# A decoder layer on one core: seven products instead of eight in the middle groups of the down projection, with sums of weight quarters made in memory

## The chip, the cores and the metric

One core of one Trainium2 chip runs the whole kernel. The metric is the device time of one execution in microseconds (us); lower is better.

## The reference, cut to what matters

The reference computes one step of a decoder layer for 512 prompt tokens and 64 sample tokens (576 in all), model width 1024, in float32: a mixer (gated linear attention and retention in parallel, four heads each), cross-attention into 256 memory tokens, and a squared-ReLU MLP of width 4096. Only the MLP's arithmetic is rearranged by the change; the mixers get transfers to issue.

```
hf = rmsnorm(x, g_pre_ffn)
x = x + rmsnorm(jnp.square(jax.nn.relu(hf @ w_up)) @ w_down, g_post_ffn)     # w_up 1024x4096, w_down 4096x1024
```

## The kernel before

Activations lie with features on the 128 partitions and the 576 tokens along the free axis, in two halves of 288. Every float32 matrix is held as a high part and a low part in the float32r format (a cast on ScalarE, `L93`, and a subtraction on VectorE, `L94`), and each product is three matmuls: high by high, low by high, high by low (`mm3`, `L251` to `L253`). A plain product of one block of 128 output features (`gemm_m`) is 8 input blocks, 3 matmuls and 2 halves: 48 matmuls of 128x128 by 288 columns.

Weights come as tiles of 128x1024 (512 KB). `plan` is the order of all of them, written out by hand. `wfetch` issues the next load on SyncE's queue (SP, `L180`) into one of four buffers `wraw`; `wsplit` makes `wh` and `wl`, of which there are three each; `wnext` keeps two split tiles ready. A load waits until the tile four before it has been split.

The kernel runs in stages: memory keys and values, mixers, mixer output projection, cross-attention, MLP. In the mixers, eight units (`UNITS`: four heads, each once for retention and once for gated attention) take eight plain products each from `plan`, and between them `tick()` advances generators in `side` that do the attention of the unit in small pieces. GpSimd (POOL) does rotary additions, causal masks, powers of -0.5 (`rs`, `L874`) and parts of the gates there.

The MLP runs in four groups `g` of 1024 hidden features. Group 0 uses plain products, up (`project`) and down (`gemm_m`). For groups 1 to 3 the up projection uses a seven-product scheme of Winograd's kind: the token halves and the parity of the feature blocks cut activations and weights in quarters, and `sevenfold` makes four output quarters out of 7 products, each 12 matmuls of 288 columns (4 blocks, 3 matmuls), instead of 8. It needs sums of activation quarters (`fsh`, `fsl`, made once by `sums_f`) and sums of weight quarters, which `begin` makes with four VectorE subtractions (`L213`) per block out of two loaded tiles. There are four blocks `b` to a group. Three accumulators are used (`acc` in pool psa, `b` in pso, `c` in psg); a product that goes on in an accumulator waits until the copy that reads its earlier content is done. `c1` and `c2` (tiles `hr`) collect the quarters, then ReLU and square on ScalarE (`L713`, `L717`, `L718`, `L722`, `L723`), then the split into `hh` and `hl`.

The down projection of groups 1 and 2 has 8 plain products, each added to `y3` in memory on chip by VectorE (`L654`). That of group 3 is in `last`, with the final norm, by halves.

The framework keeps the data's order but may place instructions on an engine's queue in another order than the one in which they are written.

Of the kernel before, what the change touches and what calls it, by code (L numbers as in the profile page):

```python
# [26 lines left out]


RING, STAY, RAW, SEVEN = 0, 1, 2, 3
# [29 lines left out]
def decoder_step(ctx, tc, xT, memT, ktc, vc, s_gla, s_ret, w_in, w_ga, w_a2, w_mix, w_xq, w_xk, w_xv, w_xo,  # L59
                 w_up, w_ups, w_down, vecs, cst, gam, y_out, mk_out, mv_out, sg_p, sr_p, sg_s, sr_s):  # L60
# [48 lines left out]
    def h2(ap):  # L109
        return ap.rearrange("p (a t) -> p a t", a=2)  # L110
# [24 lines left out]
    def whole(w, b0=0):  # L135
        return [t for b in range(4) for t in wtiles(w, b0 + b)]
# [9 lines left out]
    def rest(ts, n):  # L146
        return ts[2 + n:6] + ts[:2]
# [15 lines left out]
    def seven(w, b0):  # L163
        return [(w[b0 + b][:, kh], SEVEN) for b in range(4) for kh in range(2)]
# [6 lines left out]
    wq = []  # L171
    units = []

    def wfetch():
        if plan and sum(m == SEVEN for _, m in raws) < 2:
            src, mode = plan.pop(0), RING
            if isinstance(src, tuple):
                src, mode = src
            raw = wp.tile([P, 1024], F32, name="wraw", bufs=N_RAW)
            nc.sync.dma_start(out=raw if len(src.shape) == 2 else raw.rearrange("p (k n) -> p k n", n=src.shape[2]), in_=src)  # L180
            raws.append((raw, mode))

    def wsplit():
        if units:
            units.pop(0)()
        elif raws:
            if raws[0][1] == SEVEN:
                begin()
                return
# [4 lines left out]
            pool = staying[-1] if mode == STAY else wp  # L194
            wh = pool.tile([P, 1024], F32R, name="wh")
            wl = pool.tile([P, 1024], F32R, name="wl")
            split(wh, wl, raw)
            ready.append((wh, wl))

    def halves(w):  # L200
        return w.rearrange("p (q n) -> p q n", q=2)

    def begin():


        while len(raws) < 2:
            wfetch()
        p0, p1 = (raws.pop(0)[0] for _ in range(2))
        t = wp.tile([P, 1024], F32, name="wraw", bufs=N_RAW)
        q0, q1, qt = halves(p0), halves(p1), halves(t)  # L210

        def minus(out, a, b):
            nc.vector.tensor_tensor(out=out, in0=a, in1=b, op=ALU.subtract)  # L213

        def ring(raw):
            wh = wp.tile([P, 1024], F32R, name="wh")
            wl = wp.tile([P, 1024], F32R, name="wl")
            split(wh, wl, raw)
            ready.append((wh, wl))

        def own(raw, o, n):
            w = wq[0][:, o:o + n], wq[0][:, o + n:o + 2 * n]
            split(*w, raw)
            ready.append(w)

        def unit_a():
            ring(p0)
            wfetch()

        units.extend([unit_a, lambda: ring(t), lambda: own(p1, 0, 1024),  # L230
                      lambda: minus(q1[:, 0], q1[:, 0], qt[:, 0]), lambda: own(q1[:, 0], 2048, 512)])
        minus(qt[:, 1], q1[:, 1], q0[:, 1])
        minus(q0[:, 1], q0[:, 1], q0[:, 0])
        minus(qt[:, 0], q1[:, 1], q0[:, 1])
        wfetch()

    def wnext(n=P):

        while sum(len(r) == 2 for r in ready) < 2 and (raws or plan):
            while not units and plan and len(raws) + sum(len(r) == 1 for r in ready) < N_RAW - 1:  # L240
                n0 = len(raws)
                wfetch()
                if len(raws) == n0:
                    break
            if not raws and not units:
                break
            wsplit()
        return [a.rearrange("p (k n) -> p k n", n=n) for a in ready.pop(0)]
# [24 lines left out]
    def sevenfold(x, p1, p5, u2, c11, c22, c12, c21):  # L273
# [11 lines left out]
        def more():  # L285
            if units:
                wsplit()

        while len(ready) < 3:
            wsplit()  # L290
# [3 lines left out]
        p1(acc)  # L294
        while units:
            wsplit()
        wd = ready.pop(0)
        prod(c, wa, 1, "S1", True)
        p5(c)
        if raws and raws[0][1] == SEVEN:  # L300
            begin()
        prod(acc, wc, 0, "S2", False)
        wsplit()
        u2(acc)
        prod(b, wb, 0, "A12", True)
        more()
        c11(b)
        prod(acc, wc, 1, "S3", False)
        c22(acc)
        prod(c, wb, 1, "S4", False)  # L310
        c12(c)
        more()
        prod(acc, wd, 0, "A22", False)
        more()
        c21(acc)
# [332 lines left out]
    xnp = ctx.enter_context(tc.tile_pool(name="xnp", bufs=2))  # L648
# [4 lines left out]
    def add(out, a, b, op=ALU.add):  # L653
        nc.vector.tensor_tensor(out=out, in0=a, in1=b, op=op)  # L654

    def sums_f():

        for j in range(4):
            c1, c2 = (hp.tile([P, 2, NH], F32, name="hr") for _ in range(2))
            for i, c in enumerate((c1, c2)):  # L660
                q = slice(2 * i, 2 * i + 2)
                add(c, f32(fh[:, q, j]), f32(fl[:, q, j]))
            yield
            add(c2[:, 1], c2[:, 0], c2[:, 1])
            add(c2[:, 0], c1[:, 0], c2[:, 0], ALU.subtract)
            add(c1[:, 0], c2[:, 1], c1[:, 0], ALU.subtract)
            add(c1[:, 1], c1[:, 1], c1[:, 0], ALU.subtract)
            yield
            split(fsh[:, 2:4, j], fsl[:, 2:4, j], c2)
            split(fsh[:, 0:2, j], fsl[:, 0:2, j], c1)  # L670
            yield

    FQ = {"A11": (fh, fl, 0), "A12": (fh, fl, 1), "A22": (fh, fl, 3),
          "S2": (fsh, fsl, 0), "S4": (fsh, fsl, 1), "S3": (fsh, fsl, 2), "S1": (fsh, fsl, 3)}

    def xf7(n):
        h, l, q = FQ[n]
        return h[:, q], l[:, q]

    y3 = None  # L680
    for g in range(4):
        hh = acta.tile([P, 4, 4, NH], F32R, name="hh", tag="xh")
        hl = acta.tile([P, 4, 4, NH], F32R, name="hl", tag="xl")

        if g == 0:
            lows = []
            for half in range(2):
# [14 lines left out]
                while lows:  # L702
                    lows.pop(0)()
            y3 = bigb.tile([P, KT, NT], F32, name="y3", tag="res")
            side.append(sums_f())
            wq.append(biga.tile([P, 4608], F32R, name="wq", tag="biga"))
        else:
            for b in range(4):
                c1, c2 = (hp.tile([P, 2, NH], F32, name="hr") for _ in range(2))

                def c22(ps):
                    add(c2[:, 1], ps, c2[:, 1])
                    nc.scalar.activation(c2[:, 1], c2[:, 1], AF.Relu)  # L713

                def c12(ps):
                    add(c1[:, 1], ps, c1[:, 1])
                    nc.scalar.activation(c1, c1, AF.Relu)  # L717
                    nc.scalar.activation(c1, c1, AF.Square)  # L718
                    split(hh[:, 0:2, b], hl[:, 0:2, b], c1)

                def c21(ps):
                    nc.scalar.activation(c2[:, 0], ps, AF.Relu)  # L722
                    nc.scalar.activation(c2, c2, AF.Square)  # L723
                    split(hh[:, 2:4, b], hl[:, 2:4, b], c2)

                sevenfold(xf7, lambda ps: nc.scalar.copy(c1[:, 0], ps), lambda ps: nc.scalar.copy(c2[:, 1], ps),
                          lambda ps: nc.scalar.copy(c1[:, 1], ps), lambda ps: add(c1[:, 0], ps, c1[:, 0]), c22, c12, c21)
        if g < 3:
            for k in range(KT):
                ps = gemm_m(quarters(hh, hl), None)  # L730
                y = h2(y3[:, k, :])
                if g == 0:
                    nc.scalar.copy(y, ps)
                else:
                    add(y, ps, y)
                tick()
            drain()

# [42 lines left out]
def mixers(tc, env):  # L781
    e = Env(env)
    nc, split, split_p, gtile, atile, gemm_m, mm3, f32, h2, tick, side = (
        e.nc, e.split, e.split_p, e.gtile, e.atile, e.gemm_m, e.mm3, e.f32, e.h2, e.tick, e.side)
# [3 lines left out]
    with ExitStack() as st:  # L788
# [103 lines left out]
        def unit(h, ret, second, finish):  # L892
# [40 lines left out]
            else:  # L933
                nc.vector.tensor_tensor(out=q2(kf), in0=ps[:, :, :256], in1=pv(em), op=ALU.mult)
                for g in range(2):
                    nc.vector.tensor_tensor(out=kd[:, g], in0=parts(ps[:, g, 256:]), in1=parts(sv(em)[:, g]), op=ALU.mult)

# [7 lines left out]

            oT = u3.tile([P, 2, NT], F32, name="oT")
# [169 lines left out]
            for m in range(2):  # L1116
# [5 lines left out]
                tick()  # L1122
            for m in range(2):
# [4 lines left out]
                tick()  # L1128

# [292 lines left out]
```

## Time and profile before

| | |
|---|---|
| time, median of 3 runs | 1206.34 us (1204.42 to 1206.52) |
| the profiled execution's own time | 1206.06 us |
| its span, first to last instruction | 1204.3 us |
| TensorE (PE) busy | 1172.6 us, 97% |
| VectorE (DVE) / ScalarE (ACT) / GpSimd (POOL) busy | 745.9 / 564.3 / 152.8 us |
| moved by DMA | 158.37 MB, mean 131 GB/s |

The profile shows one execution. Times are in us unless marked ns; PEclk is the clock granted to TensorE in tenths of full speed; a DMA share is the busy share of the 16 DMA engines. Matmuls overlap each other, so the duration of one (some 295 ns) is more than the distance between two.

### The profile page before, as it was taken

To read this page: it belongs to the slowest core of one execution; us is meant where nothing else is said; L and a number is where in the kernel's file an instruction comes from. 1 tells how busy PE (TensorE), PEld (TensorE's weight loads), DVE (VectorE), ACT (ScalarE), POOL (GpSimd) and SP (SyncE) were. 2 spreads that over 40 slices of the span, in tenths; PEclk is the share of its full clock that TensorE was granted. 3 is DMA by queue.
4 is the path that set the end of the run, shared out by engine and by line. 5 is a ranking of instruction groups with operands and counts; after the bars stand their busy time and mean duration, and the time that the engine had idled before them with its cause. 6 is when DMAs were issued, how large, how long until landed. Compare 5 with 4: busy or idle time off the path is not lost.

```text
span 1204.3 us, 21958 instructions
## 1 busy us (share of the span) xinstructions
PE 1172.6 (97%) x9006; PEld 1140.8 (95%) x9006; DVE 745.9 (62%) x1332; ACT 564.3 (47%) x992; POOL 152.8 (13%) x165
## 2 busy tenths in 40 slices
PE   8999999999999999999999999999999999999995
PEld 7999999999999999999999877989999999999995
DVE  6756556565756575658677544686847457555665
ACT  6624455533544344434565444556437316415652
POOL 0621213131312231221001000000000000000000
PEclk9999999999999999999999999999999999999998
DMA  7852324242324242422644676654322322422641
GB/s 268 277 195 90 125 70 130 79 136 80 127 80 127 88 128 71 142 75 91 213 150 138 232 252 233 196 160 127 105 71 87 107 70 65 129 71 70 199 145 60
DMA packets 65621, 158.37 MB, mean 131 GB/s; under 512 B 5648, under 2 KB 34448, under 8 KB 65392
## 3 DMA queue, kind: packets, MB, share of 16 engines
q1 hardware_dynamic: 65520, 156.96, 40.9%
q8 instruction: 71, 1.16, 0.4%
q14 instruction: 30, 0.25, 0.1%
HBM read 140.68 MB, written 16.25 MB: 130 GB/s over the span
## 4 chain that ended last, share of the span: by engine, by line
PE 86%; DVE 6%; DMA 3%; ACT 3%; issue 1%; POOL 1%; SPq 0%; POOLq 0%; DVEq 0%; ACTq 0%
PE psg L252 23%; PE psg L251 23%; PE psg L253 23%; PE psa L281 4%; PE psg L281 2%; PE psa L251 1%; DVE wl L94 1%; PE psa L252 1%; PE psa L253 1%; PE pso L281 1%; DMA wraw<-in_w_xo 1%; PE pso L1241 1%; DMA wraw<-in_w_down 1%; PE psa L1084 1%; ACT wh L93 1%; DVE res L526 1%
## 5 line engine op out<-in xcount | busy, mean ns | idle before, releaser
L251 PE MATMUL psg<-xh,wh 128*128 128x288 f32 x1296 | 386.6, 298 | 3.2 <-ACT wh L93 3.2
L252 PE MATMUL psg<-xh,wl 128*128 128x288 f32 x1296 | 383.6, 296 | 2.5 <-DVE wl L94 2.5
L253 PE MATMUL psg<-xl,wh 128*128 128x288 f32 x1296 | 383.1, 296 | 0.0
L94 DVE TENSOR_TENSOR wl<-wraw,wh 128x1024 fp32r<-128x1024 f32 x197 | 243.8, 1238 | 89.9 <-ACT wh L93 88.9
L93 ACT CAST wh<-wraw 128x1024 fp32r<-128x1024 f32 x197 | 206.9, 1051 | 164.5 <-PE psg L253 104.6
L251 PEld LDWEIGHTS psg<-xh,wh 128*128 128x128 f32 x1296 | 244.3, 189 | 5.5 <-ACT wh L93 4.1
L252 PEld LDWEIGHTS psg<-xh,wl 128*128 128x128 f32 x1296 | 244.6, 189 | 3.3 <-DVE wl L94 3.2
L253 PEld LDWEIGHTS psg<-xl,wh 128*128 128x128 f32 x1296 | 244.4, 189 | 0.1
L251 PE MATMUL psg<-hh,wh 128*128 128x288 f32 x512 | 151.9, 297 | 0.7 <-DVE y L760 0.6
L252 PE MATMUL psg<-hh,wl 128*128 128x288 f32 x512 | 150.7, 295 | 0.3 <-DVE wl L94 0.3
L253 PE MATMUL psg<-hl,wh 128*128 128x288 f32 x512 | 150.7, 295 | 0.0
L251 PEld LDWEIGHTS psg<-hh,wh 128*128 128x128 f32 x512 | 96.1, 188 | 1.6 <-issue 1.1
L252 PEld LDWEIGHTS psg<-hh,wl 128*128 128x128 f32 x512 | 96.1, 188 | 0.6 <-DVE wl L94 0.6
L253 PEld LDWEIGHTS psg<-hl,wh 128*128 128x128 f32 x512 | 96.1, 188 | 0.0
L333 POOL TENSOR_TENSOR rs<-ms,mhalf 96x3 f32<-96x3 f32 (+1 forms) x11 | 11.0, 1000 | 527.4 <-DVE ms L326 527.4
L942 ACT COPY vt<-psg 128x512 f32<-128x512 f32 x16 | 9.4, 586 | 78.2 <-PE psg L253 78.2
L874 POOL TENSOR_TENSOR rs<-mv,mhalf 128x1 f32<-128x1 f32 x48 | 29.8, 621 | 112.6 <-DVE mv L869 64.5
L654 DVE TENSOR_TENSOR y<-psg,y 128x576 f32<-128x576 f32 x16 | 12.1, 758 | 50.4 <-PE psg L253 50.4
L944 DVE COPY vd<-psg 128x128 f32<-128x128 f32 x32 | 7.8, 286 | 56.0 <-ACT vt L942 56.0
L251 PE MATMUL psg<-bh,wh 128*128 128x288 f32 x128 | 38.9, 304 | 1.6 <-ACT wh L93 1.1
L252 PE MATMUL psg<-fh,wl 128*128 128x288 f32 x128 | 38.8, 303 | 0.9 <-DVE wl L94 0.9
L251 PE MATMUL psg<-fh,wh 128*128 128x288 f32 x128 | 39.0, 305 | 0.3 <-ACT fh L93 0.2
(324 smaller groups left out, 2400.2 us busy)
## 6 DMA issues: line engine op xcount, KB each, us to landing
wraw<-in_w_in SPq DMA_DIRECT2D x64, 512.0 KB, 3.6
wraw<-in_w_down SPq DMA_DIRECT2D x38, 512.0 KB, 3.7
wraw<-in_w_ups SPq DMA_DIRECT2D x24, 512.0 KB, 3.7
wraw<-in_ktc SPq DMA_DIRECT2D x16, 512.0 KB, 4.4
wraw<-in_vc SPq DMA_DIRECT2D x16, 512.0 KB, 5.2
wraw<-in_w_xq SPq DMA_DIRECT2D x14, 512.0 KB, 4.5
wraw<-in_w_xo SPq DMA_DIRECT2D x14, 512.0 KB, 5.2
wraw<-in_w_up SPq DMA_DIRECT2D x14, 512.0 KB, 4.5
```

Source lines behind the costliest of these rows:

```text
L93: nc.scalar.copy(hi, src)
L94: nc.vector.tensor_tensor(out=lo, in0=src, in1=f32(hi), op=ALU.subtract)
L251: nc.tensor.matmul(out, ah, bh, start=first, stop=False)
L252: nc.tensor.matmul(out, al, bh, start=False, stop=False)
L253: nc.tensor.matmul(out, ah, bl, start=False, stop=last)
L281: nc.tensor.matmul(out, s[:, q, k], m[:, k], start=first and k == i == 0, stop=k == 3 and i == 2, skip_group_check=True)
L333: nc.gpsimd.tensor_tensor(out=rs[:t, :n], in0=ms, in1=mhalf[:t, :n], op=ALU.pow)
L526: nc.vector.tensor_tensor(out=res[:, kk, c], in0=y[:, kk], in1=rj, op=ALU.add)
L654: nc.vector.tensor_tensor(out=out, in0=a, in1=b, op=op)
L874: nc.gpsimd.tensor_tensor(out=rs[:t], in0=mv[:t], in1=mhalf[:t, 0:1], op=ALU.pow)
L1084: nc.tensor.matmul(U[:, j * 256:(j + 1) * 256], kst[g][:, 2 * bp + j, :], vst[g], start=True, stop=True)
L1241: nc.tensor.matmul(acc[rows, :256], x(h), w[:, h], start=first, stop=last, skip_group_check=True, tile_position=(0, 32 * h))
```

## The change

The down projection of groups 1 and 2 uses `sevenfold` too: four blocks of seven products each, with the hidden layer in the place of the activations. For that the up projection of these groups keeps the hidden layer as quarters (`ha`, `fh[:, 2]`) and makes its four sums with `pairs`, block by block, into `hh` and `hl`.

The sums of weight quarters are no longer made on VectorE. The host lays out 20 blocks (`N_SEV`) as four plain quarters each (`w_sev`). Out of them the kernel makes three sums per block in memory (`t_sev`), two blocks at a time: by 40 copies from memory to memory on SP's queue, and 40 adding transfers (`accum_op`) on POOL's queue, 512 KB each. `sums()` issues them; it is called four times in each mixer unit, 32 calls in all. For ten pairs of blocks, which start at the calls in `SUMS_AT`, `SUM_STEPS` says how many calls later each of the eight transfers is issued. A block of `sevenfold` then loads seven quarters of 256 KB (four tiles, the last one half full and in a pool of its own) and splits them.

The order of products in `sevenfold` is now A11, S1, S2, S4, S3, A12, A22; with `late`, for the first block of a down projection, A12 comes right after A11. The added sums have other signs than before. The diff, cut:

```diff
+N_SEV = 20
+SUMS_AT = (2, 4, 6, 8, 10, 12, 15, 17, 19, 21)
+SUM_STEPS = (0, 0, 2, 2, 4, 6, 8, 10)
...
+    def seven(b0):
+        out = []
+        for n in range(b0, b0 + 4):
+            g, i = n // 2, n % 2
+            b = [w_sev[q, n] for q in range(4)]
+            t1, t2, t4 = t_sev[g]
+            out += [((b[0], t1[i]), RING), ((t2[0, i], t2[1, i]), RING), ((b[2], b[3]), RING), ((t4[i],), LAST)]
+        return out
...
     for g in range(1, 4):
-        plan += seven(w_ups, 4 * (g - 1))
-        plan += whole(w_down, 4 * g) + (rest(whole(w_down, 12), 0) if g == 3 else [])
+        plan += seven(8 * (g - 1))
+        plan += seven(8 * g - 4) if g < 3 else whole(w_down, 4) + rest(whole(w_down, 4), 0)
+    steps = {}
+    for g, at in enumerate(SUMS_AT):
+        b11, b12, b21, b22 = (w_sev[q, 2 * g:2 * g + 2] for q in range(4))
+        t1, t2, t4 = t_sev[g]
+        for n, (dst, src, plus) in zip(SUM_STEPS, (
+                (t1, b11, 0), (t2[1], b12, 0), (t1, b12, 1), (t2[1], b22, 1),
+                (t2[0], t1, 0), (t2[0], b22, 1), (t4, t2[0], 0), (t4, b21, 1))):
+            steps.setdefault(at + n, []).append((dst, src, plus))
+    clock = [0]
+    def sums():
+        for dst, src, plus in steps.pop(clock[0], ()):
+            if plus:
+                nc.gpsimd.dma_start(out=dst, in_=src, accum_op=ALU.add, max_dma_last_dim=8192)
+            else:
+                nc.sync.dma_start(out=dst, in_=src)
+        clock[0] += 1
...
-    def sevenfold(x, p1, p5, u2, c11, c22, c12, c21):
+    def sevenfold(x, c1, c2, done1, done22, done21, late=False):
...
         while len(ready) < 3:
-            wsplit()
+            wmore()
...
+        def c11():
+            prod(b, wb, 0, "A12", True)
+            add(c1[:, 0], b, c1[:, 0])
         prod(acc, wa, 0, "A11", True)
+        nc.scalar.copy(c1[:, 0], acc)
+        if late:
+            c11()
+        prod(c, wa, 1, "S1", True)
+        nc.scalar.copy(c2[:, 1], c)
+        wmore()
         wd = ready.pop(0)
         prod(acc, wc, 0, "S2", False)
+        nc.scalar.copy(c1[:, 1], acc)
+        wmore()
+        prod(c, wb, 1, "S4", False)
+        add(c1[:, 1], c, c1[:, 1], ALU.subtract)
         prod(acc, wc, 1, "S3", False)
+        add(c2[:, 1], c2[:, 1], acc, ALU.subtract)
+        done22()
+        wmore()
+        if not late:
+            c11()
+        done1()
+        wmore()
         prod(acc, wd, 0, "A22", False)
+        done21(acc)
...
+    def pairs(c1, c2, sh, sl):
+        add(c2[:, 1], c2[:, 0], c2[:, 1], ALU.subtract)
+        add(c2[:, 0], c1[:, 0], c2[:, 0], ALU.subtract)
+        split(sh[:, 2:4], sl[:, 2:4], c2)
+        add(c1[:, 0], c2[:, 1], c1[:, 0], ALU.subtract)
+        add(c1[:, 1], c1[:, 1], c1[:, 0])
+        split(sh[:, 0:2], sl[:, 0:2], c1)
...
+            def relu2(c, ps=None):
+                nc.scalar.activation(c, c if ps is None else ps, AF.Relu)
+                nc.scalar.activation(c, c, AF.Square)
+            def done22():
+                relu2(c2[:, 1])
+                if not plain:
+                    split(fh[:, 2, b], fl[:, 2, b], c2[:, 1])
+            def done1():
+                relu2(c1)
+                split(*((hh[:, 0:2, b], hl[:, 0:2, b]) if plain else (ha[:, 0, :, b], ha[:, 1, :, b])), c1)
+            def done21(ps):
+                relu2(c2[:, 0], ps)
+                if plain:
+                    split(hh[:, 2:4, b], hl[:, 2:4, b], c2)
+                else:
+                    pairs(c1, c2, hh[:, :, b], hl[:, :, b])
+            sevenfold(xf7, c1, c2, done1, done22, done21)
+        if plain:
+            break
+        for b in range(4):
+            c1, c2 = (hp.tile([P, 2, NH], F32, name="hr") for _ in range(2))
+            y = [y3[:, 2 * b:2 * b + 2, hc(half)] for half in range(2)]
+            def done21(ps):
+                nc.scalar.copy(c2[:, 0], ps)
+                add(y[1], y[1], c2)
+            sevenfold(xh7, c1, c2, lambda: add(y[0], y[0], c1), lambda: None, done21, b == 0)
```

## Rows read from the trace of the kernel before

**Rows 1.** The page: the span and the 40 slices.

```profile
span 1204.3 us, 21958 instructions
PE 1172.6 (97%) x9006; PEld 1140.8 (95%) x9006; DVE 745.9 (62%) x1332; ACT 564.3 (47%) x992; POOL 152.8 (13%) x165
PEclk9999999999999999999999999999999999999998
DMA  7852324242324242422644676654322322422641
```

**Rows 2.** Windows: stretch, its length, busy us (instructions) by engine, clock, DMA share, GB/s.

```profile
101.90:560.80 458.90, 458.15 (x3588) 448.42 (x3587) 286.82 (x665) 204.62 (x412) 104.61 (x110) 1.00 0.34 103
896.90:942.60 45.70, 45.26 (x338) 44.79 (x337) 31.55 (x42) 30.14 (x51) 0.00 (x0) 1.00 0.34 104
942.60:993.80 51.20, 51.20 (x387) 51.06 (x386) 21.79 (x25) 11.68 (x15) 0.00 (x0) 1.00 0.23 73
```

**Rows 3.** The chain that ended last, group 1 of the MLP: start, us, what.

```profile
896.86 1.59 PE psa L281 x12
898.45 1.60 PE psg L281 x12
...
941.02 1.60 PE psa L281 x12
993.78 1.60 PE psa L281 x12
```

**Rows 4.** Waits of PE, 860 to 1140 us: total, times, longest.

```profile
PE psa L281 <- ACT hr L726: 1.0, 3, 0.4
```

**Rows 5.** Groups by shape, ACT and DVE, 890 to 1140 us: busy, mean ns | idle before.

```profile
L93 ACT CAST wh<-wraw 128x1024 fp32r<-128x1024 f32 x42 | 44.3, 1054 | 75.6 <-PE psg L253 50.1 <-issue 10.4 <-PE psa L281 8.0
L93 ACT CAST hh<-hr 128x576 fp32r<-128x576 f32 x24 | 14.8, 667 | 0.0
L717 ACT ACTIVATE hr<-hr 128x576 f32<-128x576 f32 x12 | 8.2, 684 | 5.1 <-DVE hr L654 5.1
L713 ACT ACTIVATE hr<-hr 128x288 f32<-128x288 f32 x12 | 5.3, 442 | 16.2 <-DVE hr L654 16.2
L726 ACT COPY hr<-psg 128x288 f32<-128x288 f32 x12 | 4.8, 404 | 3.6 <-PE psg L281 3.6
L93 ACT CAST wq<-wraw 128x512 fp32r<-128x512 f32 x11 | 6.9, 625 | 8.8 <-DVE wraw L213 8.8
...
L94 DVE TENSOR_TENSOR wl<-wraw,wh 128x1024 fp32r<-128x1024 f32 x42 | 51.3, 1224 | 25.3 <-ACT wh L93 25.3
L213 DVE TENSOR_TENSOR wraw<-wraw 128x512 f32<-128x512 f32 x41 | 28.3, 691 | 1.2
L94 DVE TENSOR_TENSOR hl<-hr,hh 128x576 fp32r<-128x576 f32 x24 | 17.1, 754 | 11.0 <-ACT hh L93 11.0
L654 DVE TENSOR_TENSOR hr<-psa,hr 128x288 f32<-128x288 f32 x12 | 5.5, 458 | 6.9 <-PE psa L281 6.9
```

**Rows 6.** Timeline of ACT in a block of the up projection.

```profile
907.43 0.68 ACT L717 ACTIVATE hr<-hr 128x576 f32<-128x576 f32 x1
908.08 0.41 ACT L722 ACTIVATE hr<-psa 128x288 f32<-128x288 f32 x1
908.39 0.68 ACT L718 ACTIVATE hr<-hr 128x576 f32<-128x576 f32 x1
```

**Rows 7.** DMA issues: KB each, median us to landing; then one tile's, min/median/max, 60 to 560 us.

```profile
wraw<-in_w_in SPq DMA_DIRECT2D x64, 512.0 KB, 3.6
wraw<-in_w_xk SPq DMA_DIRECT2D x8, 512.0 KB, 6.3
...
DMA to landing us min/median/max: 3.4/3.6/6.6
```

**Rows 8.** Timelines in the mixers: SP loads, POOL's and ACT's rows of one unit.

```profile
127.47 43.50 SPq L180 DMA_DIRECT2D wraw<-in_w_in  x7
...
161.89 0.29 POOL L965 TENSOR_SCALAR_AFFINE_SELECT sm<-sm 128x128 f32<-128x128 f32 x1 [17.04 <-ACT sm L964]
173.51 0.55 POOL L874 TENSOR_TENSOR rs<-mv,mhalf 128x1 f32<-128x1 f32 x1 [1.80 <-DVE mv L872]
...
180.35 0.38 ACT L1017 COPY oT<-psa 128x256 f32<-128x256 f32 x1 [1.21 <-PE psa L1016]
```

**Rows 9.** Groups: the longest POOL operation of the mixers; SP's load waits follow.

```profile
L890 POOL TENSOR_TENSOR t<-t,t 128x576 f32<-128x576 f32 x8 | 19.2, 2398 | 35.4 <-DVE t L889 35.4
SPq L180 <- DVE wl L94: 619.5, 148, 12.2
```

**Rows 10.** The chain that ended last, mixers: one product of every unit, two units apart.

```profile
233.24 0.55 PE pso L1079 x8
...
357.58 0.55 PE pso L1079 x8
```

More of the change, by code (lines that the diff above doesn't have):

```diff
@@ L170, in decoder_step @@
+    clock = [0]
[6 more added lines that the diff above has]
+        clock[0] += 1
     raws, ready, staying = [], [], []
-    wq = []
-    units = []
+    wdp = []
     def wfetch():
-        if plan and sum(m == SEVEN for _, m in raws) < 2:
+        if plan:
             src, mode = plan.pop(0), RING
-            if isinstance(src, tuple):
+            if isinstance(src, tuple) and isinstance(src[1], int):
@@ L178, in wfetch @@
                 src, mode = src
             raw = wp.tile([P, 1024], F32, name="wraw", bufs=N_RAW)
-            nc.sync.dma_start(out=raw if len(src.shape) == 2 else raw.rearrange("p (k n) -> p k n", n=src.shape[2]), in_=src)
+            if isinstance(src, tuple):
+                for i, t in enumerate(src):
+                    nc.sync.dma_start(out=raw[:, i * 512:(i + 1) * 512], in_=t)
+            else:
+                nc.sync.dma_start(out=raw if len(src.shape) == 2 else raw.rearrange("p (k n) -> p k n", n=src.shape[2]), in_=src)
@@ L193, in wsplit, with wmore @@
                 return
[L194 to L197, printed above, removed]
+            n = 512 if mode == LAST else 1024
+            pool = wdp[0] if mode == LAST else staying[-1] if mode == STAY else wp
+            wh = pool.tile([P, n], F32R, name="wh")
+            wl = pool.tile([P, n], F32R, name="wl")
+            split(wh, wl, raw[:, :n])
             ready.append((wh, wl))
[L200 to L206, printed above, removed]
+    def wmore():
+        while plan and len(raws) < N_RAW - 1:
             wfetch()
[L208 to L235, printed above, removed]
+        wsplit()
     def wnext(n=P):
         while sum(len(r) == 2 for r in ready) < 2 and (raws or plan):
-            while not units and plan and len(raws) + sum(len(r) == 1 for r in ready) < N_RAW - 1:
-                n0 = len(raws)
+            while plan and len(raws) + sum(len(r) == 1 for r in ready) < N_RAW - 1:
                 wfetch()
-                if len(raws) == n0:
-                    break
-            if not raws and not units:
+            if not raws:
                 break
@@ L663, in sums_f @@
             yield
[L664 to L667, printed above, removed]
+            pairs(c1, c2, fsh[:, :, j], fsl[:, :, j])
             yield
[L669 to L674, printed above, removed]
+    SQ = {"S2": 0, "S4": 1, "S3": 2, "S1": 3}
     def xf7(n):
-        h, l, q = FQ[n]
-        return h[:, q], l[:, q]
+        return (fsh[:, SQ[n]], fsl[:, SQ[n]]) if n in SQ else tuple(
+            t[:, {"A11": 0, "A12": 1, "A22": 3}[n]] for t in (fh, fl))
     y3 = None
@@ L683, in decoder_step, with xh7 @@
         hl = acta.tile([P, 4, 4, NH], F32R, name="hl", tag="xl")
+        plain = g in (0, 3)
+        ha = None if plain else biga.tile([P, 2, 2, 4, NH], F32R, name="ha", tag="biga")
+        def xh7(n):
+            if n in SQ:
+                return hh[:, SQ[n]], hl[:, SQ[n]]
+            return (fh[:, 2], fl[:, 2]) if n == "A22" else (ha[:, 0, n == "A12"], ha[:, 1, n == "A12"])
         if g == 0:
@@ L703, in decoder_step @@
                     lows.pop(0)()
+            xns.close()
+            wdp.append(ctx.enter_context(tc.tile_pool(name="wdp", bufs=1)))
             y3 = bigb.tile([P, KT, NT], F32, name="y3", tag="res")
             side.append(sums_f())
[L706 to L727, printed above, removed]
@@ L728, in decoder_step @@
-        if g < 3:
-            for k in range(KT):
[L730 to L735, printed above, removed]
+            for k in range(KT):
+                nc.scalar.copy(h2(y3[:, k, :]), gemm_m(quarters(hh, hl), None))
                 tick()
             drain()
+            continue
+        for b in range(4):
[14 more added lines that the diff above has]
+                    split(hh[:, 2:4, b], hl[:, 2:4, b], c2)
+                else:
+                    pairs(c1, c2, hh[:, :, b], hl[:, :, b])
+            sevenfold(xf7, c1, c2, done1, done22, done21)
@@ L739, in decoder_step @@
+        if plain:
+            break
+        for b in range(4):
+            c1, c2 = (hp.tile([P, 2, NH], F32, name="hr") for _ in range(2))
+            y = [y3[:, 2 * b:2 * b + 2, hc(half)] for half in range(2)]
[3 more added lines that the diff above has]
+            sevenfold(xh7, c1, c2, lambda: add(y[0], y[0], c1), lambda: None, done21, b == 0)
     res2 = fsp.tile([P, KT, NT], F32, name="res2", tag="fsh")
@@ L1122, in unit @@
                 tick()
+            sums()
             for m in range(2):
@@ L1128, in unit @@
                 tick()
+            sums()
             def finish():
@@ L1398 @@
         "w_xv": np.ascontiguousarray(x["w_xv"][0].reshape(2, 4, P, 4, 256).transpose(3, 2, 0, 1, 4)), "w_xo": blocks(x["w_xo"][0]),
[L1399 to L1400 removed]
+        "w_up": blocks(wu[:, :1024]),
+        "w_sev": np.concatenate([sevens(wu[:, 1024:2048]), sevens(wd[1024:2048]), sevens(wu[:, 2048:3072]),
+                                 sevens(wd[2048:3072]), sevens(wu[:, 3072:])], axis=1),
+        "w_down": np.concatenate([blocks(wd[:1024]), blocks(wd[3072:])]),
         "vecs": np.ascontiguousarray(vecs), "cst": const,
@@ L1410 @@
         args.append(nc.dram_tensor(f"in_{n}", a.shape, mybir.dt.from_np(a.dtype), kind="ExternalInput").ap())
+    t_sev = [[nc.dram_tensor(f"t_sev{g}{i}", s + [2, P, 512], F32, kind="Internal").ap() for i, s in enumerate(([], [2], []))]
+             for g in range(N_SEV // 2)]
     outp = [nc.dram_tensor(f"out_{n}", s, F32, kind="ExternalOutput").ap() for n, s in outs.items()]
     with tile.TileContext(nc) as tc:
-        decoder_step(tc, *args, gam, *outp)
+        decoder_step(tc, *args, gam, t_sev, *outp)
     r = run_bass_kernel_spmd(nc, [ins], core_ids=[0]).results[0]
```

51 lines of the change are left out of this document (12 added, 39 removed).

## The prediction

> **What bounds the kernel now.** I read the page first. TensorE is busy in every slice and its clock is full nearly throughout [rows 1], so what counts is how many matmuls there are and where PE waits. Next the windows: in the mixers (101.9 to 560.8 us) PE is busy for 458.15 of 458.90 us, in a down projection of the middle groups for 51.20 of 51.20 [rows 2]. Then the chain that ended last, for the pace: a product of seven is 12 matmuls in 1.60 us, 133 ns each, and the plain down projection of group 1 lasts from 942.62 (941.02 + 1.60) to 993.78, 51.16 us for its 8 x 48 = 384 matmuls, 133.2 ns each [rows 3]. So both forms run at one pace, and a matmul removed here gives back 133.2 ns, if nothing else becomes late. The waits of PE in the MLP come to 1.0 us in 3 places, all for ScalarE's copy that frees an accumulator [rows 4]. VectorE and ScalarE are busy for 31.55 and 30.14 of 45.70 us in the four blocks of an up projection, 7.9 and 7.5 per block of 11.2 [rows 2]. They are not the bound, but not far off. Last I read what the mixers leave free: the DMA engines are busy for 0.34 at 103 GB/s there, POOL for 104.6 of 458.9 us [rows 2].
>
> The profiled execution took 1206.06 us with a span of 1204.3; the median of the runs is 1206.34. My sum starts from 1206.06, and the 0.28 between them is below what I can tell.
>
> **The down projections.** Before: 384 matmuls in each of two groups. After: 4 blocks x 7 products x 12 = 336. Removed: 2 x 48 = 96, times 133.2 ns = **-12.8 us** [rows 3]. The up projections keep their 84 matmuls per block.
>
> **The way from an up to a down projection.** In the plain form half 0 comes first and reads only what was split before product A22. The new down projection begins with A11, whose fourth quarter of matmuls needs the last block's `c1`, finished only after A12. From A12's last matmul: 0.16 until its result is out (295 - 133 ns), add 0.46, ReLU 0.68, square 0.68 (as ReLU), cast 0.67 [rows 5], four hand-overs that I estimate at 0.05 from the gaps between such rows: high part after 2.85 us, low part 0.80 later, 3.65. PE has A22 (1.60) and three quarters of A11 (1.20) to do, 2.80, and its third matmul of the fourth quarter, 0.27 later, wants the low part. So even with empty queues PE waits 0.6 to 0.7 us. If a weight split is just ahead of it on ScalarE (1.05) and on VectorE (1.22) and one more cast (0.67) [rows 5], it waits 3.7. I take 2.2, the middle, because both queues are four fifths full in these blocks (below). Two transitions: **+4.4** (1.4 to 7.4). The sums of the last block are late next: A22's result, ReLU, square, two adds and a cast take 0.16 + 0.40 + 0.44 + 0.92 + 0.67 + 0.3 = 2.9 us, the low part 3.7, and `late` puts A12 before S1, so that they have 1.6 + 1.6 + 1.2 = 4.4. Covered; without `late` the cover would be 2.8 and cost about 1 each time.
>
> **VectorE and ScalarE in the up blocks of groups 1 and 2.** The four subtractions `L213` go (4 x 0.69). New are a third cast and low part for the sums and one for `fh[:, 2]`. Durations of one block [rows 5], ScalarE: casts of weights 3 x 1.05 + 0.63, copies 3 x 0.40, five more operations of 288 at 0.44 or 0.40 (2.2), five of 576 at 0.68 (3.4) = 10.6; consecutive ones overlap by about 0.1 (908.08, 0.41 long, the next at 908.39 [rows 6]), so some 9.1. VectorE: 3 x 1.22 + 0.69 + 8 x 0.46 + 3 x 0.75 = 10.3, as it stands some 9.2 after the same overlap. Both are below 11.2, so PE stays the bound: cost 0 at the lower end. The cover gone is rival two. In the down blocks both have less than 8.
>
> **Loads of the MLP.** 1.75 MB per block of 11.2 us against 1 MB: 164 GB/s. The mixers' row gives 103 / 0.34 = 303 GB/s for full engines [rows 2], so a share of 0.54. A load is issued when the tile four before is split, one tile per 2.8 us, and lands after 3.6 [rows 7]; it has some 8 us. Cost 0; for each us beyond 8, up to one per block.
>
> **The mixers.** `sums()` is called every 15.5 us: two units take 357.58 - 233.24 = 124.3 us [rows 10], eight calls. 40 copies are added on SP's queue, 40 adding transfers on POOL's. No row shows either kind; they are bounded as follows.
>
> *DMA engines.* 0.524 MB at 303 GB/s is 1.73 us of all 16 engines. Copies: 40 x 1.73 = 69 us. An adding transfer holds them for 1.73 (a load) to 6.3 us (as if the 6.3 us to landing of the slowest loads of 512 KB were all engine time [rows 7]). I take twice a load, 3.46, nearer to the load, since it reads two operands and writes one. The most crowded stretch is calls 6 to 18, 186 us with 22 copies and 20 adds: 38 + 69 = 107 us, 0.58 of it, with 0.34 for the old traffic 0.92. It fits. The Trainium skill (Collectives: The Full Stack, The bandwidth ceiling) states the same: an add in the DMA engine reads two sources and ran at about half the rate of a copy. No run here shows it yet; by it the sum is the one made here.
>
> *What waits behind them.* A copy that reads a sum stands on SP two calls (31 us) behind the add that makes it, and while SP waits no weight load is issued. But weights are early: a unit has eight tiles in 62.2 us, so a load is issued four tiles, 31 us, before its use (SP's loads wait for the split four before [rows 9]; seven of them take 43.5 us [rows 8]), less 3.6 to land [rows 7] and 2.3 to split: 25 us to spare. Cost 0.
>
> *POOL.* One adding transfer holds POOL's queue for 0.4 us (an SP issue) to 2.4 (its longest operation, `L890` [rows 9]). Calls one and two of a unit fall in an idle stretch of 17.04 us [rows 8]. In calls three and four the norm's `rs` is queued behind: the first starts at 173.51, and the transposes that need it are read at 180.35, so some 5 us are to spare [rows 8]. Counting the schedule, these calls carry 2, 3, 4, 2, 1 and 2, 3, 2, 1 adds. At 2.4 each, those of three and four exceed 5 us by 2.2, 4.6 and 2.2: +9. At 0.4: nothing. I take **+1**, near the low end.
>
> **Sum.** 1206.06 - 12.8 + 4.4 + 1 = **1198.7 us**; its own range 1194.7 (1.4, 0) to 1209 (7.4, 9).
>
> **Rivals.**
> 1. *No stalls at all.* The transitions hide behind products that the framework orders better. 1206.06 - 12.8 = 1193.3. For it: PE waits in the up blocks today only 1.0 us in all [rows 4]. Against: the chain above is longer than its cover even with empty queues. 0.13.
> 2. *ScalarE's queue becomes the bound in the middle up blocks (slower).* If the last block's `pairs` stood ahead of the next block's copy of A11 as written, that copy would wait for ReLU, square, four adds, two casts and a low part, 0.16 + 0.40 + 0.44 + 1.84 + 1.34 + 0.75 + 0.4 = 5.3 us, and end at 5.7, while PE gets to S2 after 3.2: 2.5 us in six blocks, +15, so 1213.7. It decides from 1.2 us per block on, where 6 x 1.2 eats the 7.4 of the forecast. Against: the queue doesn't follow the text. `L722`, written after `L718` and the cast, stands between `L717` and `L718` when its product is ready [rows 6]. 0.10, of which 0.02 ends at no change.
> 3. *The adding transfers fill the DMA engines (slower).* At 6.3 us each, calls 6 to 18 need 38 + 126 = 164 us where 0.66 x 186 = 123 are free: 41 late, less the 25 to spare: +16, so 1214.7. It decides from about (123 + 25 + 7.4 - 38) / 20 = 5.9 us per add on. For it: adds and loads would share engines that are a third busy already. The Trainium skill (DMA: Bandwidth & Descriptors, Issuing engines are not separate DMA queues) says that they do whatever engine issues them. Against: no load in the mixers took longer than 6.6 us to land, three times its engine time [rows 7]. 0.11.
> 4. *The copies run on few engines (slower).* Their outermost extent is 2, a load's is 128 partitions. On 2 of 16 engines a copy lasts 8 x 1.73 = 13.8 us; 22 of them are 304 us in a stretch of 186, and SP's loads stand behind on these two: 118 - 25 = +93, so some 1292. The Trainium skill (DMA: Bandwidth & Descriptors, Why a DMA increments its semaphore by 16 and not by 1) states that the slowest extent above 1 sets the number of engines, which would be this case if the extents reach the queue as written; no run here shows it. Against: both ends are contiguous, and could be cut in 16. 0.04.
> 5. *The gain is eaten by small things* (POOL at 9, transitions at 7.4, set-up of POOL's queue that no row shows): 1209 at worst, 1205 to 1207 likelier: no change. 0.05.
>
> **How the numbers follow.** The forecast has 0.57. A difference of 0.2%, 2.4 us, is about what can be told from no change here. Faster: 0.57 + 0.13 = 0.70. Same: 0.05 + 0.02 = 0.07. Slower: 0.08 + 0.11 + 0.04 = 0.23. The range for 8 in 10 runs from 1193 to 1213.5: it leaves out some of rival 1 below (0.03), and above rival 4 and some two thirds of the slower ends of rivals 2 and 3 (0.04 + 0.13), whose prices lie at its edge. If the likeliest case holds, 1194.7 to 1203.
>
> **What the new profile would show.** 8910 matmuls instead of 9006. A middle down projection of 44.8 us plus its stall, 0.7 to 3.7, placed in the fourth quarter of A11 of its first block and released by ScalarE's cast or VectorE's low part. Up blocks of 11.2 us with ScalarE and VectorE at 9 to 10 (wrong, if PE waits for the copy `L726`'s successor in every block). The mixers' length as before within 2 us, with a DMA share of 0.6 to 0.9 in their middle; wrong, if PE waits there for `wh`, if SP waits for an add, or if `rs` is late on POOL. The prediction fails if the mixers grow by more than 4 us or the two down projections save less than 8.

## The result, and the profile after

| | us |
|---|---|
| before, median on the same chip | 1206.43 (1204.42 to 1206.88) |
| changed, median of 4 runs | 1278.05 (1275.86 to 1280.23) |
| ratio | 1.0601, 95% interval 1.0582 to 1.0620: **slower** |
| forecast | 1198.7, range 1193.0 to 1213.5 |

The forecast was wrong by 79 us, and wrong in sign. The page of the changed kernel, its span, engines, clock and DMA slices, to be held against [rows 1] (its lines have moved: casts and low parts are `L96` and `L97`, loads `L211` and `L213`, copies from memory to memory `L197`, adds `L195`, state stores `L1116`, `rs` `L893`):

```profile
span 1275.5 us, 22240 instructions
PE   8999999878887988999999998989999999999995
PEclk9999999989888899999999998999999999999998
DMA  8784547276465475845555556665432555554652
```

PE's row has eights and sevens from slice 8 to 16, and the granted clock falls with it. Windows of the mixers, of the up and of the down projection of the first middle group (columns as in [rows 2]):

```profile
101.90:644.70 542.80, 489.85 (x3586) 466.83 (x3585) 285.94 (x665) 204.75 (x413) 131.18 (x148) 0.94 0.57 160
981.66:1026.46 44.80, 44.80 (x339) 44.80 (x338) 33.75 (x52) 34.07 (x63) 0.00 (x0) 1.00 0.45 142
1026.46:1071.88 45.42, 45.42 (x339) 44.86 (x338) 30.43 (x43) 23.47 (x38) 0.00 (x0) 1.00 0.52 163
```

The MLP went as forecast or better: a down projection takes 45.42 us where it took 51.20 [rows 2], and PE waits in neither stretch. The whole loss is in the mixers. They take 542.80 us instead of 458.90, **+83.9**, for the same matmuls: idle time grew from 0.75 to 52.95 us, and busy time by 31.7 us (489.85 - 458.15), at a mean clock of 0.94 instead of 1.00. So PE stood still for 52 us, and its clock, granted at 0.84 where it stood still most (310 to 362 us, below), took 32 more. Everything outside the mixers gave back 71.6 - 83.9 = -12.3.

```profile
310.00:362.00 52.00, 39.31 (x257) 36.16 (x255) 21.75 (x51) 18.37 (x33) 7.88 (x9) 0.84 0.39 102
```

Who makes PE wait? Its longest waits in the mixers (total, times and longest), then those of SP's queue for states, after and before:

```profile
PE psg L246 <- ACT wh L96: 14.8, 7, 6.6
PE psg L247 <- DVE wl L97: 11.7, 9, 3.0
PE psa L1105 <- DVE on L897: 5.9, 4, 2.7
```

```profile
SPq L1116 <- DVE sn L1113: 171.3, 11, 46.7
SPq L1116 <- DVE sn L1111: 78.1, 4, 36.8
```

```profile
SPq L1095 <- DVE sn L1090: 19.9, 4, 5.0
SPq L1095 <- DVE sn L1092: 15.6, 8, 2.4
```

Half of PE's idle time, 26.5 of 52.9 us, is waits for split weights (`wh` and `wl`); the rest is short waits for small operations of the attention. Before, all waits of PE in the mixers came to 0.8 us. SP waits up to 46.7 us in one piece for a new state `sn` that it is to store; before, 5.0 at most. SP's timeline shows what stands where:

```profile
206.37 5.41 SPq L213 DMA_DIRECT2D wraw<-in_w_in  x2
211.87 0.39 SPq L1097 DMA_DIRECT2D s<-in_s_gla  x1
212.36 0.49 SPq L197 DMA_DIRECT2D t_sev<-t_sev  x1
243.98 7.85 SPq L1116 DMA_DIRECT2D out_sgs<-sn  x2
...
253.71 0.58 SPq L213 DMA_DIRECT2D wraw<-in_w_in  x1
```

Between 211.78 and 253.71 us no weight load is issued: after a state load and a copy, the next entry of the queue is a store whose `sn` isn't ready, and the loads stand behind it. Before, no two loads in a row were issued more than 12.8 us apart in the mixers; here it is up to 50.3.

These late loads are not what PE waits for, though. If loads and casts are put side by side in their order, each load of the mixers had landed at least 2.2 us before ScalarE began to cast its tile (17.5 before the change). Of the waits of these casts in the mixers only this one is put down to a load:

```profile
ACT wh L96 <- DMA wraw<-in_w_in: 1.5, 1, 1.5
```

ScalarE and PE 20 us after the long wait of SP, what stands in brackets being what the engine waited for:

```profile
275.79 0.62 ACT L100 CAST qh<-t 128x512 fp32r<-128x512 f32 x1 [10.69 <-DVE t L933]
276.32 1.04 ACT L96 CAST wh<-wraw 128x1024 fp32r<-128x1024 f32 x1
```

```profile
277.41 0.61 PE L246 MATMUL psg<-xh,wh 128*128 128x288 f32 x1 [6.64 <-ACT wh L96]
```

The cast of a weight stands behind a cast that had to wait 10.69 us for VectorE; PE waits for it. The weight itself, issued at 253.71, had landed at 262.3. Nothing here waits for a transfer of the sums. The queues have another *order* than before.

### The profile page after: what moved, and what is told of

Its sections match the earlier page's. It is cut to its first block, busy times and chain, and to the rows that moved or that the text cites. A ratio compares the mean times of both kernels' runs of the same rounds, so it can differ in the third digit from the quotient of the medians.

```text
span 1275.5 us, 22240 instructions
## 1 busy us (share of the span) xinstructions
PE 1193.3 (94%) x8910; PEld 1147.8 (90%) x8910; DVE 757.4 (59%) x1372; ACT 596.2 (47%) x1069; POOL 179.8 (14%) x205
## 4 chain that ended last, share of the span: by engine, by line
PE 80%; DVE 9%; DMA 3%; ACT 3%; issue 3%; POOL 2%; POOLq 0%; SPq 0%; DVEq 0%; ACTq 0%
PE psg L247 18%; PE psg L248 17%; PE psg L246 17%; PE psa L276 10%; PE psg L276 5%; PE pso L276 3%; DVE wl L97 2%; PE psa L246 1%; ACT wh L96 1%; PE psa L248 1%; PE psa L247 1%; POOL rs L893 1%; DMA wraw<-in_w_xo 1%; PE pso L1264 1%; DVE res L525 1%
## 5 line engine op out<-in xcount | busy, mean ns | idle before, releaser
L97 DVE TENSOR_TENSOR wl<-wraw,wh 128x1024 fp32r<-128x1024 f32 x237 | 281.9, 1192 | 137.4 <-ACT wh L96 136.6
L96 ACT CAST wh<-wraw 128x1024 fp32r<-128x1024 f32 x237 | 238.7, 1012 | 133.4 <-PE psa L276 46.3
L246 PE MATMUL psg<-hh,wh 128*128 128x288 f32 x256 | 76.0, 297 | 0.7 <-DVE y L779 0.6
L247 PE MATMUL psg<-hh,wl 128*128 128x288 f32 x256 | 75.4, 295 | 0.3 <-DVE wl L97 0.3
L248 PE MATMUL psg<-hl,wh 128*128 128x288 f32 x256 | 75.4, 295 | 0.0
L893 POOL TENSOR_TENSOR rs<-mv,mhalf 128x1 f32<-128x1 f32 x48 | 32.4, 675 | 125.4 <-DVE mv L888 66.7
L246 PEld LDWEIGHTS psg<-hh,wh 128*128 128x128 f32 x256 | 48.1, 188 | 1.2 <-issue 1.1
L247 PEld LDWEIGHTS psg<-hh,wl 128*128 128x128 f32 x256 | 48.0, 188 | 0.6 <-DVE wl L97 0.6
L248 PEld LDWEIGHTS psg<-hl,wh 128*128 128x128 f32 x256 | 48.0, 188 | 0.2 <-DVE hl L97 0.2
L248 PE MATMUL psg<-bl,wh 128*128 128x288 f32 x128 | 38.6, 301 | 0.0
L247 PE MATMUL psg<-bh,wl 128*128 128x288 f32 x128 | 38.4, 300 | 0.0
```

What stands on the lines that cost most here:

```text
L96: nc.scalar.copy(hi, src)
L97: nc.vector.tensor_tensor(out=lo, in0=src, in1=f32(hi), op=ALU.subtract)
L246: nc.tensor.matmul(out, ah, bh, start=first, stop=False)
L247: nc.tensor.matmul(out, al, bh, start=False, stop=False)
L248: nc.tensor.matmul(out, ah, bl, start=False, stop=last)
L893: nc.gpsimd.tensor_tensor(out=rs[:t], in0=mv[:t], in1=mhalf[:t, 0:1], op=ALU.pow)
```

## The experiments

Three theories, as the expectations name them. **A**: the framework, which orders each engine's queue by its own estimate of times, takes the copies in rows of 32 KB for long and so puts weight loads, and the work that hangs on them, late; the loss is in this order. **B** and **C** put it to the transfers themselves on the chip, with the adds in the first place. What follows compares the queues of the built kernels too: of PE's 8623 entries, 8348 of the changed kernel stand in the same sequence as in the kernel without sums (the longest that both have), and 8614 when the copies have rows of 8 KB. That is an order on paper; times come from the chip.

**1. The sums left out (e1).** No copy and no add; the four tiles are loaded from plain quarters (so sums are replaced by plain weights, and the MLP's numbers are others).

```diff
-            out += [((b[0], t1[i]), RING), ((t2[0, i], t2[1, i]), RING), ((b[2], b[3]), RING), ((t4[i],), LAST)]
+            out += [((b[0], b[1]), RING), ((b[2], b[3]), RING), ((b[2], b[3]), RING), ((b[1],), LAST)]
...
-        for dst, src, plus in steps.pop(clock[0], ()):
+        for dst, src, plus in ():
```

> None of the 80 transfers that make sums in memory is issued; the tiles of the seven products are loaded from plain quarters instead (the same loads in number and size), so the weights of groups 1 to 3 are not the right sums. All theories expect the MLP's own gain here: twelve microseconds less the two waits between an up and a down projection, 1194 to 1200 us. If it comes out above 1206, the MLP is to blame, not the transfers.

Measured: 1192.52 us, ratio 0.9879 (0.9856 to 0.9903), 14 us less than before and 1.5 below the range expected. That is what the MLP's part of the change is worth.

**2. Copies alone (e3), adds alone (e4).** In e3 the adds are left out (the sums are then unfinished); in e4 the copies, but for four that fill scratch buffers once, into which the adds go (and the MLP reads plain quarters).

```diff
 e3
-            if plus:
-                nc.gpsimd.dma_start(out=dst, in_=src, accum_op=ALU.add, max_dma_last_dim=8192)
-            else:
+            if not plus:
                 nc.sync.dma_start(out=dst, in_=src)
 e4
+        if clock[0] == 0:
+            for i in range(4):
+                nc.sync.dma_start(out=t_sev[i][0], in_=w_sev[0, 0:2])
...
-                nc.gpsimd.dma_start(out=dst, in_=src, accum_op=ALU.add, max_dma_last_dim=8192)
-            else:
-                nc.sync.dma_start(out=dst, in_=src)
+                nc.gpsimd.dma_start(out=t_sev[clock[1] % 4][0], in_=src, accum_op=ALU.add, max_dma_last_dim=8192)
+                clock[1] += 1
```

> The 40 copies stay as they are, the 40 adding transfers are left out (the sums are incomplete). Theory A, the order of the queues: the framework orders SP's and the other engines' queues by its own estimate of when loads land, the long copies of 16 rows of 32 KB upset that, weight loads end up behind stores that wait for the mixers' results; then this is as slow as the changed kernel, 1265 to 1285. Theory B, the DMA engines are full: copies hold them for 40 x 1.37 = 55 us of the 172 that copies and adds take by their packets, so about a third of the loss remains, some 1220. Theory C, POOL's queue is held by the adds (40 x 0.83 us): nothing of the loss remains, 1195 to 1200.

> The 40 adding transfers stay, of the same size and at the same calls, but go in turn into four buffers that are filled once; the 40 copies are left out, and the tiles are loaded from plain quarters (sums left out). Theory A: 1195 to 1202, the queues are as in the kernel before. Theory B: two thirds of the loss remain, 40 x 2.92 = 117 of 172 us of engine time, some 1245 to 1255. Theory C: all of it remains, 1265 to 1285.

Measured, one time each: copies alone 1272.37, adds alone 1226.22. The copies carry nearly the whole loss, as A says. But A's value for the adds was missed by 24 us. Windows of e4:

```profile
102.00:154.00 52.00, 39.99 (x268) 36.58 (x268) 26.59 (x63) 14.99 (x32) 17.08 (x23) 0.80 0.95 206
154.00:206.00 52.00, 50.05 (x387) 48.97 (x387) 31.11 (x64) 28.08 (x55) 21.91 (x30) 1.00 1.04 263
206.00:258.00 52.00, 46.13 (x340) 45.30 (x339) 24.15 (x52) 20.97 (x35) 12.40 (x12) 0.93 0.58 154
258.00:310.00 52.00, 52.00 (x410) 50.86 (x409) 35.47 (x83) 23.14 (x54) 15.60 (x17) 1.00 0.36 114
```

The DMA share is 0.95 and 1.04, then back at its old level: without copies that pace them, the adds were placed at the front, 36 of the 40 issued between 94 and 223 us and not spread over the calls where `sums()` is written, and filled the DMA engines. Part of it is e4's own: POOL stood there for 77.6 us at adds that waited for an earlier transfer, since 40 of them share four scratch buffers. The bunch is a second effect, which the changed kernel doesn't show (none of its windows of 52 us in the mixers is above 0.77). The changed kernel with all its adds is 5.7 us slower than e3, which has none.

**3. Everything, copies in rows of 8 KB (e7).**

```diff
-                nc.sync.dma_start(out=dst, in_=src)
+                nc.sync.dma_start(out=dst, in_=src, max_dma_last_dim=8192)
```

> All 80 transfers with all their bytes; the copies are only cut into 64 rows of 8 KB instead of 16 of 32 KB. Theory A: the plan of the queues no longer takes them for long, weight loads keep their place, 1195 to 1202. Theory B: the same bytes on the same engines, 1265 to 1285. Theory C: the adds hold POOL as before, 1265 to 1285. A variant of B, in which single packets of 32 KB hold an engine for 1.37 us each and so delay loads, would give 1195 to 1205 here too; it has to be told from A otherwise.

Measured: 1222.07 us, ratio 1.0138 (1.0113 to 1.0163): 56 us of the loss are gone with one argument, 30 over e1 are left, about what the adds cost in e4. So A's value was missed here too, by 20 us, and that of B and C by 43. Its windows show the same bunch:

```profile
102.00:154.00 52.00, 45.46 (x334) 43.02 (x333) 29.54 (x74) 20.15 (x41) 16.04 (x19) 0.93 1.02 294
154.00:206.00 52.00, 49.88 (x381) 48.51 (x379) 26.30 (x66) 24.12 (x52) 13.56 (x19) 0.97 1.01 279
206.00:258.00 52.00, 47.89 (x352) 47.23 (x351) 23.66 (x51) 22.63 (x39) 20.24 (x22) 0.97 0.97 286
258.00:310.00 52.00, 47.69 (x354) 45.88 (x355) 31.13 (x75) 19.50 (x43) 19.88 (x20) 0.97 0.83 226
```

How a full DMA reaches PE in e7 is seen on three timelines, POOL, VectorE and PE:

```profile
192.28 0.81 POOL L195 DMA_DIRECT2D t_sev<-in_w_sev  x1 [7.99 <-DMA t_sev<-in_w_sev]
192.85 0.83 POOL L893 TENSOR_TENSOR rs<-mv,mhalf 128x1 f32<-128x1 f32 x1
```

```profile
188.55 0.14 DVE L891 TENSOR_SCALAR mv<-mv 128x1 f32<-128x1 f32 x1
193.72 0.48 DVE L899 TENSOR_SCALAR on<-psa,rs 128x256 f32<-128x256 f32 x1 [5.02 <-POOL rs L893]
```

```profile
194.26 0.51 PE L1105 MATMUL psa<-vs,ks 128*128 128x256 f32 x2 [2.12 <-DVE on L899]
```

`mv` is ready at 188.69, but POOL stands for 7.99 us at an add whose predecessor has not landed, `rs` comes 4 us late behind it, then `on`, then PE. Of 17 us of such waits of PE between 101 and 320 us, 13 are for `on`. So an add costs POOL's queue not only the 0.81 us of its issue, but also the wait for what it reads.

**4. Spread as written (e8), and order against transfer (e10, e11).** e8: rows of 8 KB, and each transfer queued behind the last instruction that the program had given its queue by then. e10: the change as it is, rows of 32 KB, with all five engines' queues in e8's order. e11: rows of 8 KB in the changed kernel's order. `ORDER` is the list of instruction numbers, engine by engine. In the traces all five engines run e10 in the sequence of e8, and e11 in that of the changed kernel, entry by entry.

```diff
 e8
+            eng = nc.gpsimd if plus else nc.sync
+            with tc.issue_after(next(i for i in reversed(nc.cur_bb.bb.instructions) if i.engine == eng.engine)):
...
 e10, e11
+        for a, b in zip(order[:-1], order[1:]):
+            if a > 0 and b > 0 and a in at and b in at:
+                tc.add_manual_dep(at[int(b)], at[int(a)].name, mybir.DependencyInfo(
+                    mybir.DependencyClass.NoSync, mybir.DependencyReason.DATA), reason="order")
```

> Copies cut to rows of 8 KB, and each copy and each add queued behind the last instruction that the program had given its queue by then, so that they come every 15.5 us as written, not in the first 200 us of the mixers. Theory 'bunched': the 30 us that the run with 8 KB rows still lost over the run without sums came because the adds and copies were issued as early as their own data allowed and held the DMA engines at a share of 0.97 to 1.02 from 102 to 258 us; spread, they need 40 x (2.92 + some 1.4) = 173 us of each engine in 460, 0.38 beside the old 0.34: share 0.6 to 0.9 in the windows, PE waits in the mixers below 6 us, 1192 to 1200. Rival 'adds cost wherever they are' (loads slowed by an adding transfer, POOL's queue held): 1213 to 1222, PE waits of 15 us or more with the share below 0.95.

> The change as it is, copies in rows of 32 KB, but every engine's instructions in the order of the run before it (8 KB rows, spread). Theory 'order': the 72 us that the rows of 32 KB cost come from the order that the framework makes when it takes these copies for long, not from the transfers: within 6 us of the run before it, 1192 to 1206. Rival 'long packets': a packet of 32 KB holds an engine 1.37 us and the loads' packets stand behind it; then the loss stays, 1240 or more, with the share far below 1.

> The converse: copies in rows of 8 KB, every engine's instructions in the order of the changed kernel. Theory 'order': as the changed kernel, 1262 to 1285, SP waiting for sn up to 40 us. Rival 'long packets': 1192 to 1225.

Measured on one chip, before there 1205.90:

| us (ratio, 95% interval) | order of e8 | order of the changed kernel |
|---|---|---|
| rows of 8 KB | 1193.48 (0.988 to 0.991) | 1275.71 (1.0562 to 1.0598) |
| rows of 32 KB | 1196.96 (0.9908 to 0.9944) | 1278.05, on another chip |

The order is worth 82 us with rows of 8 KB and, across two chips, 81 with rows of 32 KB. The longer row costs 3.5 us in the one order; in the other the two ratios (1.0580 and 1.0601) can't be told apart. e11 has SP's long waits again, e10 has not (SP's queue in e11; windows of e11, then of e10, 310 to 362 us):

```profile
SPq L1420 <- DVE sn L1417: 170.9, 11, 46.8
```

```profile
310.00:362.00 52.00, 40.62 (x268) 37.46 (x266) 21.70 (x50) 18.15 (x32) 7.88 (x9) 0.84 0.41 104
```

```profile
310.00:362.00 52.00, 51.12 (x396) 50.08 (x395) 28.80 (x59) 24.61 (x45) 16.31 (x18) 1.00 0.90 261
```

With the DMA engines at 0.90, PE is busy and at full clock; at 0.41 in the other order it stands for 11 us of 52. e8 is faster than both kernels, and its crowded windows are about those expected:

```profile
258.00:310.00 52.00, 52.00 (x409) 50.86 (x408) 32.70 (x74) 16.26 (x33) 16.58 (x18) 1.00 0.77 230
310.00:362.00 52.00, 51.91 (x403) 51.10 (x402) 30.07 (x63) 25.86 (x48) 16.10 (x18) 1.00 0.93 266
362.00:414.00 52.00, 52.00 (x406) 51.43 (x405) 31.94 (x72) 18.94 (x40) 19.44 (x20) 1.00 0.86 235
```

**5. Which half of the spreading, and the order of products (e12 to e14).** e13 paces only the adds, e14 only the copies, both with rows of 8 KB; e12 is e8 without `late`.

```diff
 e12
-            sevenfold(xh7, c1, c2, lambda: add(y[0], y[0], c1), lambda: None, done21, b == 0)
+            sevenfold(xh7, c1, c2, lambda: add(y[0], y[0], c1), lambda: None, done21)
```

> Copies in rows of 8 KB; only the adds are queued behind the instruction ahead of them on POOL, the copies are free to go early. By the theory 'bunched' it is the adds, 117 of the 173 us of each engine, that fill the DMA engines; the 10 first copies of each kind come early, the others wait for adds: 1193 to 1203. By the rival, that any bunch of these transfers on SP stops the weight loads, 1205 to 1222.

> The converse: only the copies are paced on SP, the adds are free on POOL. Each add needs a copy first, so their data spread them too: 1193 to 1203, if nothing but the bunch costs. If adds placed by the framework hold POOL's queue while they wait for a transfer, rs and ks come late: 1203 to 1215, with PE waits for on.

> The spread kernel with the order of products unchanged in the first block of a down projection (A12 ahead of A22, not right after A11). The prediction's chain: A11 with only S1 behind it waits for c1 by 0.7 to 3.7 us and S1 for the sums, so 2 to 9 us more than the spread kernel, with PE waits in the fourth quarter of A11 at both transitions. Rival 'reordered': the framework fills the wait with quarters of other products whose operands are ready, as it does with A12's quarters in the spread kernel: 1192 to 1196 and PE waits below 0.5 us there.

Measured: e13 1194.36 (0.9866 to 0.9931), e14 1192.54 (0.9868 to 0.9924), e12 1194.78 (0.9885 to 0.9932), against 1205.27 before on that chip. Either half is enough: adds wait for copies and later copies for adds, so that one half can pace the other. That this is why is argued. e14's feared wait of PE for `on` isn't there (0.3 us), although POOL stands at adds for up to 9.9 us, and although the DMA engines are nearly as full as in e7 for 52 us:

```profile
258.00:310.00 52.00, 52.00 (x410) 50.86 (x409) 33.19 (x75) 15.64 (x34) 14.88 (x18) 1.00 0.96 273
```

So neither a full window nor an add that waits need reach PE. In e7 an add stood ahead of an `rs` that PE needed soon. And `late` is worth nothing that can be measured: e12 has no wait of PE between 840 and 1150 us.

## Why the prediction was wrong

**Removed matmuls: right.** 8910 are left of 9006, and 96 x 133.2 ns = 12.8 us is what the rest of the kernel gave back (12.3 in the changed kernel, 12.4 in e8, 14.0 in e1).

**The way from an up to a down projection, +4.4: too much, it is 0.** The chain to `c1` was not the error. What I took for fixed was that PE sits at A11's last quarter. PE's timeline of the changed kernel at the first transition:

```profile
1027.37 0.29 PE L276 MATMUL psa<-ha,wh 128*128 128x288 f32 x1
1027.50 0.29 PE L276 MATMUL pso<-ha,wh 128*128 128x288 f32 x1
...
1028.56 0.29 PE L276 MATMUL pso<-ha,wh 128*128 128x288 f32 x1
1028.84 0.40 PE L276 MATMUL psa<-ha,wh 128*128 128x288 f32 x1
```

After nine matmuls of A11 (psa) come nine of A12 (pso), 1.3 us, and only then the quarters that need the last block. e12 fills the same gap with nine of S1. This is rival 1, in the MLP: its condition, "products that the framework orders better", held.

**VectorE and ScalarE in the up blocks: right**, 33.75 and 34.07 us in four blocks of 11.2, 8.4 and 8.5 each; PE doesn't wait, rival 2 is out. **Loads of the MLP: right**, share 0.45 and 0.52 against 0.54.

**The mixers' DMA engines: right in size.** The sum gave 0.92 in the crowded stretch; spread as written (e8) it is 0.77 to 0.93, with PE waiting less than 1 us. An add takes 2.93 us of each engine against 3.46 assumed (POOL's queue of the changed kernel; 0.092 x 1275.5 / 40). A copy has 16 packets of 1.37 us each, so 1.37 of each engine on average, against 1.73 assumed. The Trainium skill (Collectives: The Full Stack, The bandwidth ceiling) says that an add, there in a collective, ran at about half the rate of a copy; 2.93 to 1.37 is 2.1, the trace agrees.

```profile
q0 software_dynamic: 3200, 20.97, 9.2%
```

**The failed step is "What waits behind them": "But weights are early ... Cost 0".** The 25 us to spare were read from a queue in which the loads stand ahead of the stores [rows 8, 9]. I let the new transfers join that queue where they are written, and left everything else in place. The framework made a new order for all engines. With it the mixers cost 83.9 us more where the sum had 1, or 72 net of what the rest gave back; that the order does it is shown by e10 and e11, in which order and rows are exchanged.

The way was not the one that this step looked at either. Loads stand behind stores that wait up to 46.7 us, and their cover shrinks, but at least 2.2 us of it are left. What PE waits for are casts and low parts that stand behind other work on ScalarE and VectorE (26.5 us), and small operations of the attention (26.4); the lower clock adds 32. The prediction named "if PE waits there for `wh`" as a sign of being wrong, and that sign came. Which queue's order costs how much is not shown, since e10 and e11 exchange all five at once.

The statement ahead of the prediction that the order may differ from the text was used for rivals 1 and 2 alone, and there for the MLP; no rival priced a new order of the mixers.

**"POOL", +1, and rival 3.** Issuing an add takes 0.83 us of POOL (the median), which would have done little. The adds do fill the DMA engines when they come at once (e4, e7: +30 to 34 us, through POOL's queue and `rs`), which is rival 3's mechanism in another place and for another reason: not 6.3 us per add, but 36 adds issued within 127 us (94.5 to 221.1 us in e4), where the calls, followed as written, spread as many over 315 (144.6 to 459.1 us in e8). The changed kernel itself doesn't show it.

**Rival 4 is out.** A copy lands in 7.3 us (the median) and has 16 packets of 1.37; on two engines eight in a row would take 11.0.

What stays open: that the framework's estimate of a transfer with rows of 32 KB is what makes the order is argued from the queues of the built kernels (the order follows the row's length), its estimate itself was not seen. Why the slow order of ScalarE and VectorE comes out as it does was not followed further. e3 and e4 were timed once each.

## What to carry to other kernels

When a framework orders the queues, a transfer that the data leave free is not issued where it is written, and its price in the framework's estimate can move everything else; a forecast has to price a new order, and after any such edit the first thing to compare is the sequence on each queue, then the times. Tie such transfers to the instruction beside them on their queue, and the plan can hold: here that, together with rows of 8 KB, turned +6.0% into -1.05%. With rows of 32 KB it was not run by itself (e10 has the whole order imposed). A slack is worth only as much as the order in which it was read, and a long wait on a queue is not yet the cause: follow what the stalled engine waits for.

## What was not expected of the hardware

DMA shares of 0.90 to 0.96 in windows of 52 us cost PE less than 1 us (e8, e10, e14). At 0.95 to 1.04 PE stood still for 2 to 12 us (e4, e7), where the adds also held POOL's queue, so the share alone doesn't decide. Packets of 32 KB instead of 8 KB cost 3.5 us in all (e10 against e8).

The granted clock has two levels, 1.2 and 2.4 GHz, 0.50 and 1.00 in these rows, and a value between them is a mean over a stretch. In the changed kernel it is 0.50 from 239.5 to 242.6 us, where matmuls of 288 columns follow each other 0.24 us apart, after PE had stood still for 1.3, 1.3 and 2.5 us within 8 us; then it is 1.00 again, and they follow 0.13 us apart. In this kernel's mixers the lower level made up 32 of the 84 us.
